# Weight blocks laid out in HBM so that each one is contiguous per partition

## The chip, the cores and the metric

The kernel runs on one core of one Trainium2 chip. Within that core five engines work side by side: TensorE (PE, with its weight loads shown apart as PEld), VectorE (DVE), ScalarE (ACT), GpSimd (POOL) and SyncE (SP). SP does no arithmetic here; it issues DMAs, and nearly all DMAs of this kernel are issued by it, in one queue. Sixteen DMA engines move the data between HBM and the core's SBUF.

The metric is the device time of one execution in microseconds. Before the change the median of three runs is 2130.68 us (2130.02 to 2132.34).

## The reference

One encoder layer is applied to two sequences of 512 tokens by 1024 channels (a prompt and a sample), all in float32:

```
x = x + 0.5 * swiglu(rms_norm(x, ffn1_norm), w_gate, w_up, w_down)     # D_FF = 2816
h = rms_norm(x, mix_norm);  proj = h @ w_in                            # w_in: 1024 x 4880
att = grouped-query attention (8 query heads, 2 key heads, 64 wide, axial rotary, QK norm)
mem = bidirectional mLSTM (4 heads, 128 wide), normed per head, times a sigmoid gate
x = x + (sigmoid(g_att) * (att @ w_up_att) + sigmoid(g_mlstm) * (mem @ w_up_mlstm)) @ w_out
x = x + 0.5 * swiglu(rms_norm(x, ffn2_norm), w_gate, w_up, w_down)
return rms_norm(x, final_norm)
```

`swiglu(x) = (silu(x @ w_gate) * (x @ w_up)) @ w_down`. Columns of `w_in` are, in order, attention q (512), k and v (256), memory q, k and v (512 each), 16 gate columns, the memory's output gate (512) and the two merge gates (1024 each).

## The kernel before

Both sequences are worked on together. The stages in order of time are: the first FFN's gate and up products (to about 440 us), its down product (to about 660 us), the mixing block for one sequence and then the other (to about 1475 us), and the second FFN, gate and up (to about 1865 us) and down (to the end).

Every product keeps float32 accuracy by splitting both operands into a high and a low float32r part and adding three products, high by high, high by low and low by high. So every weight block that is loaded is split once, by an ACT copy (the high part) and a DVE subtraction (the low part), before TensorE can use it.

The gate and up products of an FFN are one 2x2 block product (gate and up against the two sequences, the contraction cut in two halves) done with seven instead of eight block products, so that sums of blocks have to be formed on DVE. The output is walked in 22 steps of 128 columns; `ORDER` (L368) fixes which. A step j takes 128 columns of the gate weight and the same 128 of the up weight. `Up.fetch` (L382) asks for both and `fetch_w` (L188) issues one DMA for each on SP, into a tile `wr` of 128 x 8 x 128 floats (512 KB); four such tiles exist. In HBM the weight is 1024 x 2816 and row-major, so that a partition's 4 KB of such a block lie in eight pieces of 512 bytes.

`gu_left_a`, `gu_left_b` and `gu_left_c` (L253 to L276) turn the two blocks into the seven left operands. The first DVE operation that needs the up block is L263. `gu_rest` (L300) runs the products of a step; each is 12 matmuls at L282. For the first seven of the 22 columns blocks two of the seven products are done early (`Up.begin`, L385) and their results are parked in HBM and fetched again at L400, so in the first 14 steps a step with 5 products alternates with one with 7. The sum at L311 (`u2 = v1 + Y`) writes a ring buffer, and TensorE's next products into the bank Y wait for it.

After every second step `Sides.even` and `Sides.odd` (L348, L353) form the seven right operands of the down product from the two steps' results. `Sides.out` (L340) splits one (L343 on ACT, L344 on DVE) and stores the high and the low part to the DRAM buffer `rbuf` by two DMAs of 256 KB (L345 and L346). With `last=True` the low part is written over the source, so that the source's ring buffer comes free only once that store has landed. L311 of the next step waits for such a buffer; this is the "DMA rbuf<-t" of the profile.

So one SP queue carries, in the order in which the program was scheduled, the stores of the sides, the loads of the next gate and up blocks, the parked results, and in the down stage the loads `rt<-rbuf` of 512 KB each (L457) and the down weights. An SP instruction that waits holds back all that stand behind it.

In the mixing block `load_w` (L208) loads and splits a weight block. `win_cols` (L693) loads 128 columns of `w_in` as 8 x 128; `tok_proj` (L645) loads two row blocks of 512 columns, or for keys and values 256 + 16 columns by two DMAs; `up_unit` (L967) loads 4 x 256 and `out_half` (L1095) 2 x 512.

```
raw = wpool.tile(shape, F32, tag="wr", bufs=4, name=nm("wr"))
for v in views:
    nc.sync.dma_start(raw[:, :, c:c + v.shape[2]], v)      # L195
...
self.v = [w.rearrange("(k p) c -> p k c", p=P) for w in (wg, wu)]
return [fetch_w(self.v[i][:, :, j * P:(j + 1) * P]) for i in which]
```

Of the kernel before, what the change touches and what calls it, by code (L numbers as in the profile page):

```python
# [16 lines left out]
P = 128  # L17
S = 512
D = 1024
KD = D // P  # L20
# [6 lines left out]
def encoder(ctx, tc, I, outs):  # L27
    nc = tc.nc
# [159 lines left out]
    def fetch_w(view):  # L188
        views = view if isinstance(view, list) else [view]
        shape = list(views[0].shape)  # L190
        shape[2] = sum(v.shape[2] for v in views)
        raw = wpool.tile(shape, F32, tag="wr", bufs=4, name=nm("wr"))
        c = 0
        for v in views:
            nc.sync.dma_start(raw[:, :, c:c + v.shape[2]], v)  # L195
            c += v.shape[2]
        return raw
# [18 lines left out]
    V_ = nc.vector  # L216
# [23 lines left out]
        pin(nc.scalar.activation(t[:, 0], src, AF.Copy))  # L240
        pin(V_.tensor_tensor(t[:, 1], src, f(t[:, 0]), op=ALU.subtract))  # L241

    def gu_fetch(wgv, wuv, j):
        cs = slice(j * P, (j + 1) * P)
        return fetch_w(wgv[:, :, cs]), fetch_w(wuv[:, :, cs])

    half = lambda r, i: r[:, i * HK_:(i + 1) * HK_, :]
    part = lambda t, i: (t[:, 0, i], t[:, 1, i])

# [120 lines left out]
    class Up:  # L370


        def __init__(self, xc, wg, wu, rb):
            self.xc, self.rb = xc, rb
            self.v = [w.rearrange("(k p) c -> p k c", p=P) for w in (wg, wu)]
            self.kept = {}
            self.ring = Rings(s=["t2"] * 3, wd=["f2"] * 2, v=["t2"] * 3, h=["t2"] * 5, o=["f2"] * 2 + ["R"] * 2)
            self.ring.rows["o"] += tables(FFN_ROWS)
            self.ring.join("x", "v", "h")
            self.ring.rows["k"], self.ring.at["k"] = self.ring.rows["o"][:2], 0  # L380

        def fetch(self, j, which=(0, 1)):  # L382
            return [fetch_w(self.v[i][:, :, j * P:(j + 1) * P]) for i in which]

        def begin(self, j, W):  # L385

# [237 lines left out]
            tabs.append((cg, sg))  # L624
        tabs.extend((tri, msk))

    w_in = I["w_in"][0]
    win_v = w_in.rearrange("(k p) c -> p k c", p=P)


    held = []
# [1 line left out]
    def go(*units):  # L633
        for load, comp in units:
            held.append((comp, load()))
            while len(held) > 1:
                c, w = held.pop(0)
                c(w)
# [3 lines left out]
            c, w = held.pop(0)  # L642
            c(w)

    def tok_proj(xh, xl, cols, kk, done):  # L645

        N = sum(n for _, n in cols)
        p = []

        def load(k0):  # L650
            return load_w([win_v[:, k0:k0 + kk, c:c + n] for c, n in cols], nc.vector)

        def comp(k0, w):
            wh, wl = w
            if not p:
                p.extend([MM(), MM(), MM(), PO()])
            for kl in range(kk):
                k = k0 + kl
                for b in range(4):
# [21 lines left out]
    def mix(s, xh, xl, before, after):  # L681

        xsrc = lambda k: (xh[:, k, :], xl[:, k, :])
# [7 lines left out]
            return T2(dtype, "f2")  # L691

        def win_cols(c0, done):  # L693
            return proj(win_v[:, :, c0:c0 + P], xsrc, KD, done)


        kv = A([P, 8, S], F32R, "kv")
# [76 lines left out]
        cs = small(96, "cs")  # L774
# [39 lines left out]
        def mem_values():  # L814
            def done(pvv):
                vm = A([P, 2, 4, S], F32R, "Vm")
                for b in range(4):
                    split(pvv[b], vm[:, 0, b, :], vm[:, 1, b, :])
                Vm.append(vm)
            return tok_proj(xh, xl, [(1792, 512)], 2, done)  # L820

        qks = {}

        def mem_qk(h, j):
            def done(pp):
                if j == 0:
                    qks[h] = wpool.tile([P, 4, S], F32R, tag="w8", bufs=4, name=nm("qk"))
                split(pp, qks[h][:, 2 * j, :], qks[h][:, 2 * j + 1, :])
            return win_cols((768, 1280)[j] + h * P, done)

        ogs = {}

        def out_gate(h):
            def done(pp):
                og = T2(F32, "ac")
                nc.scalar.activation(og, pp, AF.Tanh, scale=0.5)
                G_.tensor_scalar(og, og, 1.0, hn[:, h:h + 1], op0=ALU.add, op1=ALU.mult)
                ogs[h] = og
            return win_cols(2320 + h * P, done)

        def q_rope(b):
            qo = rope_apply(qraw[b], rq[0][:, b * 8:(b + 1) * 8], tabs[0], b).rearrange("p (h e) -> p h e", e=DA)
# [6 lines left out]
                nc.scalar.activation(qT[:, g * 4:g * 4 + 4, b * P:(b + 1) * P],  # L849
                                     p.rearrange("p (h t) -> p h t", t=P), AF.Copy)  # L850

        go(*tok_proj(xh, xl, [(512, 256), (2304, 16)], 2, kv_done))
        go(*tok_proj(xh, xl, [(0, 512)], 2, q_done), mem_qk(0, 0))
        yield None
        box()
        gates()
# [90 lines left out]
        def att_gate(d):  # L947
            def done(pp):
                nc.scalar.activation(mg[:, d, :], pp, AF.Tanh, scale=0.5)
            return win_cols(2832 + d * P, done)  # L950

        queue.extend(att_gate(d) for d in range(KD))
        queue.extend(out_gate(h) for h in range(2))
# [11 lines left out]
        wups = {}  # L965

        def up_unit(part, d, src, done):  # L967
            def load():
                if d % 2 == 0:
                    wv = I[("w_up_att", "w_up_mlstm")[part]][0].rearrange("(k p) c -> p k c", p=P)  # L970
                    wups[part, d // 2] = load_w(wv[:, :, d * P:(d + 2) * P], nc.vector)

            def comp(_):
                wu = wups[part, d // 2]
                cl = slice((d % 2) * P, (d % 2 + 1) * P)
                done(proj_w(wu[0][:, :, cl], wu[1][:, :, cl], lambda k: (src[:, k, 0, :], src[:, k, 1, :]), 4))
            return load, comp
# [8 lines left out]
        def mem_gate(d):  # L986
            def done(pp):
                t = ths[d] = T2()
                nc.scalar.activation(t, pp, AF.Tanh, scale=0.5)
            return win_cols(3856 + d * P, done)  # L990

        def merge_mem(d):
            def done(pu):
# [95 lines left out]
        yield None  # L1089


        wov = I["w_out"][0].rearrange("(k p) c -> p k c", p=P)
        rows = A([P, 2, 4, S], F32, "rows") if s else None

        def out_half(h):  # L1095

            p = []

            def comp(k0, w):
                if not p:  # L1100
                    p.extend([MM(), MM(), MM(), PO()])
                for k in (k0, k0 + 1):
                    for b in range(4):
                        bs = slice(b * P, (b + 1) * P)
                        for i, (a, w_) in enumerate(((mh, w[0]), (mh, w[1]), (ml, w[0]))):
                            nc.tensor.matmul(p[b], a[:, k, bs], w_[:, k - k0, :],  # L1106
                                             start=(k == 0 and i == 0), stop=(k == KD - 1 and i == 2))
                if k0 + 2 < KD:
                    return
                for b in range(4):  # L1110
                    xt = rows[:, h, b, :] if s else T2()
                    nc.sync.dma_start(xt, xbuf[s][:, h, b, :])
                    V_.scalar_tensor_tensor(xt, p[b], 0.5, xt, op0=ALU.mult, op1=ALU.add)
                    nc.sync.dma_start(x2buf[s][:, h, b, :], xt)
                    square(xt, ssq2[s][:, h, b:b + 1])

            return [(lambda k0=k0: load_w(wov[:, k0:k0 + 2, h * S:(h + 1) * S], V_), lambda w, k0=k0: comp(k0, w))
                    for k0 in range(0, KD, 2)]

        go(*out_half(0), *out_half(1))  # L1120
# [5 lines left out]
    for _ in range(8):  # L1126
# [3 lines left out]
    rbuf = [[[dpool.tile([P, 2, S], F32, name=f"rbuf{n}_{j}_{m}") for m in range(7)] for j in range(NF // 2)]  # L1130
            for n in range(2)]
    xnbuf = dpool.tile([P, KD, S], F32, name="xnbuf")
    raws = [A([P, 4, D], F32, "raw") for _ in range(2)]
    xc = [None] * 7
    up = Up(xc, I["ffn1_w_gate"][0], I["ffn1_w_up"][0], rbuf[0])
# [96 lines left out]
    for k in range(HK_):  # L1232
# [3 lines left out]
        for t, kk, bank in ((x1l, k, PS), (x1u, k + HK_, PT)):  # L1236
            p = turn(1, kk, [bank])
# [50 lines left out]
    xc = [None] * 7  # L1288
# [14 lines left out]
    rows1 = next(m1)  # L1303


    up = Up(xc, I["ffn2_w_gate"][0], I["ffn2_w_up"][0], rbuf[1])
    raw0 = up.fetch(0)
    W = [gu_left_a(raw0[0])]
    up.begin(0, W[0])
# [68 lines left out]
        'ffn2_w_gate', 'ffn2_w_up', 'ffn2_w_down', 'final_norm']  # L1378


# [17 lines left out]
```

## Time and profile before

| | us |
|---|---|
| median of three runs | 2130.68 (2130.02 to 2132.34) |
| the profiled execution | 2131.81 |
| its span, first to last instruction | 2130.0 |
| TensorE matmul busy | 2071.1 (97%) |
| TensorE weight loads busy | 1689.2 (79%) |
| DVE busy | 1579.5 (74%) |
| ACT busy | 968.5 (45%) |
| DMA queue of SP, share of 16 engines' span | 50.6% |

The profile shows one execution. A row of a timeline gives start and length in us, engine, source line, operation and tiles (`out<-in`, buffer numbers left out); in brackets stands the idle time of the engine just before it and what ended it. The chain of waits is followed back from the last instruction: at each point it names the work, or the DMA, that the next piece waited for. The list of waits adds up, for each engine and line, how long it stood idle for which releaser (us in total, times, longest). The list of DMA issues gives tile and source, count, size and the median time from issue to landing. Stretches ("windows") give busy time with the number of instructions in brackets, for PE, PEld, DVE, ACT and POOL, then the granted clock, the DMA share and GB/s.

### The profile page before, as it was taken

The numbers are of one execution on the slowest core, as the hardware profiler recorded it, in microseconds if no ns is written. First come the engines' busy times: TensorE is split into PE (matmuls) and PEld (weight loads), VectorE is DVE, ScalarE is ACT, GpSimd is POOL, SyncE is SP. The second block draws the span as 40 slices with busy tenths as digits, with TensorE's granted clock in tenths as the row PEclk, the third lists the DMA queues.
The fourth block names the chain that finished last, engine by engine and source line by source line (L and its number), as shares of the span: only waits on it lengthen the run. The fifth ranks groups of instructions, "written<-read, shape, count | busy, mean of one in ns | idle before, by whom it ended". The sixth has DMA issues, their size and how long they took to land.

```text
span 2130.0 us, 26826 instructions
## 1 busy us (share of the span) xinstructions
PE 2071.1 (97%) x9472; PEld 1689.2 (79%) x9472; DVE 1579.5 (74%) x2817; ACT 968.5 (45%) x1739; POOL 104.1 (5%) x110
## 2 busy tenths in 40 slices
PE   6999999999999999999999999999999999999997
PEld 5877788888888777878887887788877778888885
DVE  7888887776696796574668755754978887786686
ACT  6534444442225466454435654544644444442223
POOL 1000000001000110100102001010000000000002
PEclk9999999999999999999999999999999999999998
DMA  8465554389765222333352232454464654479753
GB/s 266 150 197 186 182 196 142 131 303 378 281 219 162 78 71 64 95 103 97 117 159 81 60 90 79 129 178 158 154 197 159 197 165 166 142 261 386 284 207 122
DMA packets 294486, 361.81 MB, mean 170 GB/s; under 512 B 17776, under 2 KB 187776, under 8 KB 293328
## 3 DMA queue, kind: packets, MB, share of 16 engines
q1 hardware_dynamic: 293760, 358.84, 50.6%
q0 software_dynamic: 592, 1.27, 0.3%
q8 instruction: 74, 1.21, 0.2%
q14 instruction: 60, 0.49, 0.1%
HBM read 255.15 MB, written 104.89 MB: 169 GB/s over the span
## 4 chain that ended last, share of the span: by engine, by line
PE 74%; DVE 10%; DMA 6%; issue 6%; ACT 4%; POOL 0%; SPq 0%; DVEq 0%; ACTq 0%; POOLq 0%
PE mm L678 14%; PE pss L282 13%; PE pst L282 8%; PE mm L523 8%; PE mm L282 7%; PE pss L523 4%; PE pst L523 4%; PE mm L662 3%; PE pso L523 3%; DMA rbuf<-t 2%; DMA wr<-in_ffn_w_up_dram 2%; PE pso L932 1%; PE mm L1106 1%; PE pso L1062 1%; DVE w L241 1%
## 5 line engine op out<-in xcount | busy, mean ns | idle before, releaser
L678 PE MATMUL mm<-xh,w 128*128 128x512 f32 x896 | 292.0, 395 | 0.0
L282 PE MATMUL pss<-xc,w 128*128 128x512 f32 x1056 | 258.4, 391 | 12.4 <-DVE t L311 12.4
L282 PE MATMUL mm<-xc,w 128*128 128x512 f32 x1056 | 256.0, 391 | 2.5 <-ACT f L291 2.4
L282 PE MATMUL pst<-xc,w 128*128 128x512 f32 x1056 | 255.4, 390 | 0.0
L282 PEld LDWEIGHTS pss<-xc,w 128*128 128x128 f32 x1056 | 196.6, 188 | 60.4 <-DVE t L311 20.0
L282 PEld LDWEIGHTS mm<-xc,w 128*128 128x128 f32 x1056 | 196.8, 188 | 46.8 <-ACT f L291 6.6
L282 PEld LDWEIGHTS pst<-xc,w 128*128 128x128 f32 x1056 | 197.3, 188 | 43.2 <-ACT t L315 2.5
L203 DVE TENSOR_TENSOR w<-wr,w 128x1024 fp32r<-128x1024 f32 (+1 forms) x112 | 135.9, 1215 | 106.0 <-ACT w L202 100.7
L678 PEld LDWEIGHTS mm<-xh,w 128*128 128x128 f32 x896 | 167.6, 188 | 32.1
L523 PE MATMUL mm<-w,rt 128*128 128x512 f32 x792 | 185.6, 390 | 1.1 <-DMA rt<-rbuf 1.1
L678 PE MATMUL mm<-xl,w 128*128 128x512 f32 x448 | 176.7, 394 | 0.0
L523 PEld LDWEIGHTS mm<-w,rt 128*128 128x128 f32 x792 | 148.4, 188 | 32.5 <-DMA rt<-rbuf 1.8
L240 ACT ACTIVATE w<-t 128x512 fp32r<-128x512 f32 x176 | 107.0, 628 | 122.8 <-DVE t L266 42.0
L202 ACT ACTIVATE w<-wr 128x1024 fp32r<-128x1024 f32 (+1 forms) x112 | 114.4, 1028 | 99.4 <-PE mm L678 29.4
L241 DVE TENSOR_TENSOR w<-t,w 128x512 fp32r<-128x512 f32 x176 | 118.0, 689 | 44.5 <-ACT w L240 41.5
L282 PE MATMUL pss<-xc,f 128*128 128x512 f32 x528 | 128.4, 392 | 0.0
L282 PEld LDWEIGHTS pss<-xc,f 128*128 128x128 f32 x528 | 98.2, 188 | 23.6 <-DVE t L319 3.6
L580 ACT ACTIVATE w<-wr 128x512 fp32r<-128x512 f32 x72 | 44.6, 631 | 132.4 <-PE pso L523 64.3
L580 ACT ACTIVATE w<-t 128x512 fp32r<-128x512 f32 x82 | 51.6, 632 | 115.9 <-PE pst L523 47.3
L678 PEld LDWEIGHTS mm<-xl,w 128*128 128x128 f32 x448 | 84.3, 188 | 15.7
L523 PE MATMUL pss<-w,rt 128*128 128x512 f32 x396 | 94.0, 389 | 0.0
L523 PE MATMUL pst<-w,rt 128*128 128x512 f32 x396 | 93.7, 389 | 0.0
(316 smaller groups left out, 3644.4 us busy)
## 6 DMA issues: line engine op xcount, KB each, us to landing
rt<-rbuf SPq DMA_DIRECT2D x154, 512.0 KB, 5.8
wr<-in_w_in_dram SPq DMA_DIRECT2D x72, 512.0 KB, 3.6
wr<-in_ffn_w_gate_dram SPq DMA_DIRECT2D x56, 512.0 KB, 5.3
rbuf<-tab SPq DMA_DIRECT2D x90, 256.0 KB, 3.2
wr<-in_ffn_w_up_dram SPq DMA_DIRECT2D x44, 512.0 KB, 4.2
rbuf<-t SPq DMA_DIRECT2D x88, 256.0 KB, 3.5
rbuf<-f SPq DMA_DIRECT2D x66, 256.0 KB, 3.2
rbuf<-R SPq DMA_DIRECT2D x64, 256.0 KB, 3.5
```

The source lines that it names most:

```text
L202: pin(nc.scalar.activation(hi, raw, AF.Copy))
L203: pin(lo_eng.tensor_tensor(lo, raw, f(hi), op=ALU.subtract))
L240: pin(nc.scalar.activation(t[:, 0], src, AF.Copy))
L241: pin(V_.tensor_tensor(t[:, 1], src, f(t[:, 0]), op=ALU.subtract))
L282: nc.tensor.matmul(p, a[:, k, :], xt[:, b, k, :], start=(first and k == 0 and i == 0), stop=(k == HK_ - 1 and i == 2), skip_group_check=True)
L523: nc.tensor.matmul(p, r[:, b, d * P:(d + 1) * P], u[:, a, :], start=(first and q == 0 and k == 0), stop=(q == len(us) - 1 and k == 2), ski ...
L580: nc.scalar.activation(hi, src, AF.Copy)
L662: nc.tensor.matmul(p[b][:, :N], a[:, k, bs], w_[:, kl, :], start=(k == 0 and i == 0), stop=(k == KD - 1 and i == 2))
L678: nc.tensor.matmul(p, a[:, k, :], b, start=(k == 0 and i == 0), stop=(k == n - 1 and i == 2))
L932: nc.tensor.matmul(po, Vst[:, kv_, hk, :], w, start=(kv_ == 0 and i == 0), stop=(kv_ == 3 and i == 1))
L1062: nc.tensor.matmul(po, vm[:, a, t, hs_], b, start=(t == 0 and n == 0), stop=(t == 3 and n == 2))
L1106: nc.tensor.matmul(p[b], a[:, k, bs], w_[:, k - k0, :], start=(k == 0 and i == 0), stop=(k == KD - 1 and i == 2))
```

## The change

The host lays the weights out anew with numpy before the program is built (`lay_out`); values are not changed. For each block that the kernel loads, the bytes of one partition become one contiguous run, and the block as a whole becomes contiguous in HBM. The loads take these blocks by index. The 256 + 16 columns of keys and values become one block of 272, so two DMAs become one. The down weights, inputs, constants and all buffers in HBM that the kernel writes itself stay as they were. `gu_fetch`, which nothing called, goes.

```
     def __init__(self, xc, wg, wu, rb):
-        self.v = [w.rearrange("(k p) c -> p k c", p=P) for w in (wg, wu)]
+        self.v = wg, wu
     def fetch(self, j, which=(0, 1)):
-        return [fetch_w(self.v[i][:, :, j * P:(j + 1) * P]) for i in which]
+        return [fetch_w(self.v[i][j]) for i in which]
...
-    w_in = I["w_in"][0]
-    win_v = w_in.rearrange("(k p) c -> p k c", p=P)
+    win_c, win_t = I["w_in_cols"], {n: I[f"w_in_{n}"] for n in ("q", "kv", "mv")}
...
-            return load_w([win_v[:, k0:k0 + kk, c:c + n] for c, n in cols], nc.vector)
+            return load_w(win_t[name][k0 // kk], nc.vector)
...
-            return proj(win_v[:, :, c0:c0 + P], xsrc, KD, done)
+            return proj(win_c[c0], xsrc, KD, done)
...
-        go(*tok_proj(xh, xl, [(512, 256), (2304, 16)], 2, kv_done))
+        go(*tok_proj(xh, xl, "kv", 272, 2, kv_done))
...
-                    wups[part, d // 2] = load_w(wv[:, :, d * P:(d + 2) * P], nc.vector)
+                    wups[part, d // 2] = load_w(I[("w_up_att", "w_up_mlstm")[part]][d // 2], nc.vector)
...
-            return [(lambda k0=k0: load_w(wov[:, k0:k0 + 2, h * S:(h + 1) * S], V_), lambda w, k0=k0: comp(k0, w))
+            return [(lambda k0=k0: load_w(wov[h, k0 // 2], V_), lambda w, k0=k0: comp(k0, w))
...
+def lay_out(given):
+    def blocks(w, rows, cols):
+        w = w.reshape(w.shape[0] // (rows * P), rows, P, w.shape[1] // cols, cols)
+        return np.ascontiguousarray(w.transpose(3, 0, 2, 1, 4))
+    for n in (1, 2):
+        for part in ("gate", "up"):
+            name = f"ffn{n}_w_{part}"
+            given[name] = blocks(given[name][0], KD, P)[:, 0]
+    w = given.pop("w_in")[0]
+    given["w_in_cols"] = blocks(np.concatenate([w[:, 768:1792], w[:, 2320:]], axis=1), KD, P)[:, 0]
+    given["w_in_q"] = blocks(w[:, :512], 2, 512)[0]
+    given["w_in_kv"] = blocks(np.concatenate([w[:, 512:768], w[:, 2304:2320]], axis=1), 2, 272)[0]
+    given["w_in_mv"] = blocks(w[:, 1792:2304], 2, 512)[0]
+    for name in ("w_up_att", "w_up_mlstm"):
+        given[name] = blocks(given[name][0], 4, 2 * P)[:, 0]
+    given["w_out"] = blocks(given["w_out"][0], 2, S)
```

In the scheduled program the order of the instructions on TensorE, ScalarE and GpSimd is the same as before. On DVE two neighbouring instructions of the mixing block's start change places (L145 and L203). On SP the order is the same but for the eight DMAs of 16 gate columns, which are gone; the semaphores that the later DMAs report on are numbered differently, since they are dealt out in turn.

More of the change, by code (lines that the diff above doesn't have):

```diff
@@ L241, in w_pair @@
         pin(V_.tensor_tensor(t[:, 1], src, f(t[:, 0]), op=ALU.subtract))
-    def gu_fetch(wgv, wuv, j):
-        cs = slice(j * P, (j + 1) * P)
-        return fetch_w(wgv[:, :, cs]), fetch_w(wuv[:, :, cs])
     half = lambda r, i: r[:, i * HK_:(i + 1) * HK_, :]
@@ L643, in flush, with tok_proj @@
             c(w)
-    def tok_proj(xh, xl, cols, kk, done):
-        N = sum(n for _, n in cols)
+    def tok_proj(xh, xl, name, N, kk, done):
         p = []
         def load(k0):
-            return load_w([win_v[:, k0:k0 + kk, c:c + n] for c, n in cols], nc.vector)
+            return load_w(win_t[name][k0 // kk], nc.vector)
         def comp(k0, w):
@@ L819, in done @@
                 Vm.append(vm)
-            return tok_proj(xh, xl, [(1792, 512)], 2, done)
+            return tok_proj(xh, xl, "mv", 512, 2, done)
         qks = {}
@@ L828, in done @@
                 split(pp, qks[h][:, 2 * j, :], qks[h][:, 2 * j + 1, :])
-            return win_cols((768, 1280)[j] + h * P, done)
+            return win_cols(4 * j + h, done)
         ogs = {}
@@ L838, in done @@
                 ogs[h] = og
-            return win_cols(2320 + h * P, done)
+            return win_cols(8 + h, done)
         def q_rope(b):
@@ L850, in q_rope @@
                                      p.rearrange("p (h t) -> p h t", t=P), AF.Copy)
-        go(*tok_proj(xh, xl, [(512, 256), (2304, 16)], 2, kv_done))
-        go(*tok_proj(xh, xl, [(0, 512)], 2, q_done), mem_qk(0, 0))
+        go(*tok_proj(xh, xl, "kv", 272, 2, kv_done))
+        go(*tok_proj(xh, xl, "q", 512, 2, q_done), mem_qk(0, 0))
         yield None
@@ L949, in done @@
                 nc.scalar.activation(mg[:, d, :], pp, AF.Tanh, scale=0.5)
-            return win_cols(2832 + d * P, done)
+            return win_cols(12 + d, done)
         queue.extend(att_gate(d) for d in range(KD))
@@ L969, in load @@
                 if d % 2 == 0:
-                    wv = I[("w_up_att", "w_up_mlstm")[part]][0].rearrange("(k p) c -> p k c", p=P)
-                    wups[part, d // 2] = load_w(wv[:, :, d * P:(d + 2) * P], nc.vector)
+                    wups[part, d // 2] = load_w(I[("w_up_att", "w_up_mlstm")[part]][d // 2], nc.vector)
             def comp(_):
@@ L989, in done @@
                 nc.scalar.activation(t, pp, AF.Tanh, scale=0.5)
-            return win_cols(3856 + d * P, done)
+            return win_cols(20 + d, done)
         def merge_mem(d):
@@ L1089, in mix @@
         yield None
-        wov = I["w_out"][0].rearrange("(k p) c -> p k c", p=P)
+        wov = I["w_out"]
         rows = A([P, 2, 4, S], F32, "rows") if s else None
@@ L1134, in encoder @@
     xc = [None] * 7
-    up = Up(xc, I["ffn1_w_gate"][0], I["ffn1_w_up"][0], rbuf[0])
+    up = Up(xc, I["ffn1_w_gate"], I["ffn1_w_up"], rbuf[0])
     xins = [I[n][0] for n in ("x_prompt", "x_sample")]
@@ L1303, in encoder @@
     rows1 = next(m1)
-    up = Up(xc, I["ffn2_w_gate"][0], I["ffn2_w_up"][0], rbuf[1])
+    up = Up(xc, I["ffn2_w_gate"], I["ffn2_w_up"], rbuf[1])
     raw0 = up.fetch(0)
@@ L1378 @@
         'ffn2_w_gate', 'ffn2_w_up', 'ffn2_w_down', 'final_norm']
+def lay_out(given):
+    import numpy as np
+    def blocks(w, rows, cols):
[13 more added lines that the diff above has]
+    given["w_out"] = blocks(given["w_out"][0], 2, S)
+    return given
 def kernel(**inputs):
@@ L1388 @@
     given = {n: _np.ascontiguousarray(inputs[n]) for n in _INS}
+    given = lay_out(given)
     given.update(host_consts())
```

## The prediction

> **What bounds the kernel now.** I read the page first, then who waited for whom, then the chain of waits in the stage that this points to.
>
> ```profile
> span 2130.0 us, 26826 instructions
> PE 2071.1 (97%) x9472; PEld 1689.2 (79%) x9472; DVE 1579.5 (74%) x2817; ACT 968.5 (45%) x1739; POOL 104.1 (5%) x110
> DMA packets 294486, 361.81 MB, mean 170 GB/s; under 512 B 17776, under 2 KB 187776, under 8 KB 293328
> q1 hardware_dynamic: 293760, 358.84, 50.6%
> ```
>
> TensorE is busy for 2071.1 of 2130.0 us, and the change takes no matmul away. A faster load can win at most what TensorE stands idle, 58.9 us, and of that only what a weight load causes. The DMA engines are half idle, so bytes per second over the whole run are not the limit; single transfers that somebody waits for are. TensorE's waits are these:
>
> ```profile
> PE pss L1147 <- DVE raw L1195: 13.7, 2, 11.3
> PE pss L282 <- DVE t L311: 12.4, 14, 2.3
> PE pst L848 <- DVE t L581: 4.4, 4, 1.8
> ...
> PE mm L523 <- DMA rt<-rbuf: 1.1, 1, 1.1
> ```
>
> The first is the norm of the inputs at the start, which needs the x rows and no weight. The third is arithmetic of the attention, as are most of those left out. The last is a load that isn't changed. The second is the gate and up stage of both FFNs: 14 waits, 12.4 us in all, for the DVE sum at L311. What that sum waits for, from the list of waits of DVE:
>
> ```profile
> DVE t L263 <- DMA wr<-in_ffn_w_up_dram: 29.7, 33, 1.8
> DVE t L311 <- DMA rbuf<-t: 14.0, 13, 2.8
> DVE R L1187 <- DMA raw<-in_x_prompt_dram: 6.3, 3, 3.4
> ```
>
> L311 waits for a store (its ring buffer must have been written out), and earlier in the same step DVE waits at L263 for the up block. The chain of waits over one such place, and SP's queue there:
>
> ```profile
> 173.85 2.73 PE pst L282 x12
> ...
> 178.81 0.68 DVE w L241
> 179.50 0.61 DVE t L344
> ...
> 180.12 4.09 DMA rbuf<-t
> ...
> 184.24 0.70 DVE t L311
> ...
> 184.98 1.19 PE pss L282 x4
> ```
>
> ```profile
> 173.20 0.41 SPq L195 DMA_DIRECT2D wr<-in_ffn_w_up_dram  x1
> ...
> 176.99 0.40 SPq L346 DMA_DIRECT2D rbuf<-t  x1
> 177.43 0.78 SPq L195 DMA_DIRECT2D wr<-in_ffn_w_gate_dram  x1
> 180.12 0.32 SPq L346 DMA_DIRECT2D rbuf<-t  x1
> ```
>
> The store issued at 180.12 takes 4.09 us. In the queue there stand ahead of it the next gate block (177.43), stores, and the up block (173.20). Both loads are of the changed kind. At 1547.74 and 1554.60 the same chain shows the two transfers one behind the other:
>
> ```profile
> 1547.74 4.30 DMA wr<-in_ffn_w_up_dram
> ...
> 1554.60 5.16 DMA rbuf<-t
> ```
>
> **The change part by part.** *Gate and up blocks (56 + 44 loads).* Each load keeps its 512 KB but its 1024 pieces of 512 bytes become 128 of 4 KB. The trace has 4 KB rows of the same total size already: the loads of `rt`. First the gate, then the up blocks, then `rt`:
>
> ```profile
> L195 SPq DMA_DIRECT2D wr<-in_ffn_w_gate_dram x56: 367/392/4948, 2.6 to 1843.2; - x56
> DMA to landing us min/median/max: 3.7/5.3/10.5
> L195 SPq DMA_DIRECT2D wr<-in_ffn_w_up_dram x44: 367/384/3274, 14.8 to 1849.8; - x44
> DMA to landing us min/median/max: 3.7/4.2/8.6
> L457 SPq DMA_DIRECT2D rt<-rbuf x154: 319/320/975, 445.5 to 2082.8; - x154
> DMA to landing us min/median/max: 3.1/5.8/10.1
> ```
>
> The medians say little, since `rt` loads come in bursts and queue behind each other. The shortest landings compare alike: 3.7 against 3.1 us, 0.6 us less a load. The start of the kernel gives a second view, where the queue is full: from 13 to 16 us it moves x rows of 4 KB, from 18.3 to 22 us weight blocks of 512-byte pieces.
>
> ```profile
> 13.00:16.00 3.00, 0.00 (x0) 0.00 (x0) 2.59 (x14) 0.78 (x1) 0.00 (x0) 1.00 1.03 410
> 18.30:22.00 3.70, 3.70 (x24) 3.57 (x23) 3.61 (x5) 3.70 (x8) 0.00 (x0) 1.00 1.16 290
> ```
>
> At 410 GB/s a block of 524,288 bytes streams in 1.28 us, at 290 in 1.81 us: 0.53 us less. So 0.6 us a load is my value; the ends are 0 (the landing is all latency; a loss is the last of the rivals) and 0.9, from the 243 GB/s that a stretch with an up block inside a step shows below (2.16 us a block, against 1.28).
>
> ```profile
> 1549.30:1551.00 1.70, 1.70 (x9) 1.39 (x9) 1.70 (x4) 0.00 (x0) 0.00 (x0) 1.00 0.91 243
> ```
>
> On the path of one wait lie two loads, the up block (by L263 and by the queue) and the gate block (by the queue ahead of the store), so 1.2 us can come off each wait, and no more than the wait itself. Of the 14 waits four are longer:
>
> ```profile
> 184.98 3.92 PE L282 MATMUL pss<-xc,w 128*128 128x512 f32 x16 [1.30 <-DVE t L311]
> 1560.52 3.92 PE L282 MATMUL pss<-xc,w 128*128 128x512 f32 x16 [2.29 <-DVE t L311]
> 1595.00 3.93 PE L282 MATMUL pss<-xc,w 128*128 128x512 f32 x16 [1.28 <-DVE t L311]
> 1629.59 3.92 PE L282 MATMUL pss<-xc,w 128*128 128x512 f32 x16 [1.39 <-DVE t L311]
> ```
>
> They keep 0.10 + 1.09 + 0.08 + 0.19 = 1.5 us, and 12.4 - 1.5 = 10.9 us go. What is late next? A pair of steps lasts 34.49 us in the worst of these stretches:
>
> ```profile
> 150.49:184.98 34.49, 33.19 (x144) 26.80 (x145) 28.12 (x44) 14.46 (x24) 0.00 (x0) 1.00 0.59 190
> ```
>
> DVE works 28.12 us of it. Even when TensorE's 33.19 us leave no gap, DVE has 5 us to spare, ACT more. So TensorE itself is next, and no new wait takes the gain.
>
> The Trainium skill, "DMA: Bandwidth & Descriptors", section "Why small descriptors are slow (HBM only)", charges a fixed 3 cycles or so to each piece, 32 bytes a cycle. By that, 512 bytes cost 19 cycles where the share of a 4 KB piece costs 16.4, so a block would stream only about 0.2 us faster, an estimate from that page; then two loads give 0.4 us a wait, at most 14 x 0.4 = 5.6 us, and 2125.1. The two stretches above speak for more.
>
> *Up blocks, early.* SP itself is held while it issues these loads, up to 4948 and 3274 ns at the start of the kernel by the rows above. Fewer pieces hold it less. Nothing of TensorE waits for SP there except through x, so I take 0. The x rows land ahead of the gate blocks in the same queue; DVE waits 6.3 us for them in three pieces, the first of 3.4 until anything can have landed. The other 2.9 bound what a lighter queue could give, and a change of sign has the same bound at most; I take 0.
>
> *Mixing block: `w_in`, `w_up_att`, `w_up_mlstm`, `w_out`.* 0.
>
> ```profile
> L203 DVE TENSOR_TENSOR w<-wr,w 128x1024 fp32r<-128x1024 f32 (+1 forms) x112 | 135.9, 1215 | 106.0 <-ACT w L202 100.7
> L202 ACT ACTIVATE w<-wr 128x1024 fp32r<-128x1024 f32 (+1 forms) x112 | 114.4, 1028 | 99.4 <-PE mm L678 29.4
> wr<-in_w_in_dram SPq DMA_DIRECT2D x8, 16.0 KB, 3.7
> ```
>
> The splits of these blocks wait for each other and, first, for TensorE to free a buffer, not for the load; matmuls at L678 cover it. Were that cover gone, a shorter load would help, not hurt. The eight small DMAs of gate columns go, with 0.4 us of SP each, which nobody waits for: 0. Their partner's rows become 2176 bytes, between sizes that the trace has. On DVE two neighbours change places (L145 and L203); one may wait for the other's 0.7 to 1.2 us, eight loads early in the block, so within 1 us either way; I take 0. The renumbered semaphores make a DMA wait for another one eight issues back, which is old by then: 0.
>
> *The sum.* The profiled execution took 2131.81 us, 1.81 beside its span; 2131.8 - 10.9 = 2120.9. It lies 1.1 above the median of the runs, 2130.68, so against that 2119.8.
>
> **The rivals.** *One load only.* If the store gains from the gate block alone, because the up block's lead is lost in the wait for L344, 0.6 us a wait remain: at most 14 x 0.6 = 8.4, less for waits that are shorter, some 7.5, and 2123. For it: in the chain at 180.12 the up load doesn't stand. Against it: the queue between 173 and 184 holds both.
>
> *All of it and the start.* With 0.9 us a load only the wait of 2.29 keeps 0.5; with the x rows' 2.9 us too, 12.4 - 0.5 + 2.9 = 14.8, and 2115.9. Against it: the x rows go first.
>
> *Nothing changes.* A load might cost what its latency and bytes cost, whatever its pieces; 0 a load, 2130.7. For it: the queue is half idle, and the 3.7 us of a lone block are more than twice the time that its bytes stream. Against it: 290 against 410 GB/s. The Trainium skill's page "DMA: Bandwidth & Descriptors", section "Specifications", puts line rate at 512 bytes and more; by that rule this case holds, and the two stretches disagree.
>
> *Slower.* Sixteen engines now read rows that lie side by side in one block of 512 KB, instead of pieces 11 KB apart. If those collide in HBM and a block lands later than 3.7 us, each load is added where it is now taken off. A block that lands 0.6 us later makes each of the 14 waits 1.2 us longer: 16.8 us, 2147.5; it decides from the point where a block lands 0.15 us later than now (14 x 0.3 = 4.2 us). Against it: x rows and `rt` lie in just that way and go at 410 GB/s.
>
> **How the numbers follow.** Forecast 0.50, one load only 0.20, all of it 0.13, nothing 0.10, slower 0.07. About 0.2%, 4.3 us, is what a measurement here can tell from no change: the first three are all faster by more, 0.83; same 0.10; slower 0.07. The range goes from the third case's 2115 to 2129, which lets in part of the case without change; what is left out is under 0.15. The forecast alone: 2117.5 to 2122.
>
> **What would show it.** Right: the shortest landing of gate and up blocks near 3.1 us; some 140,000 packets fewer than the 294486 of now (56 gate, 44 up and 56 blocks of `w_in`, 896 each); DVE's 29.7 us at L263 and 14.0 at L311 mostly gone; TensorE's 12.4 us at L311 under 2.5; the other waits of TensorE the same. Wrong: landings that stay at 3.7; a store in front of L311 that still takes 4 to 5 us; TensorE's waits moving to another line, above all to products at L282 that wait for ACT or for a weight split that comes late.

## The result and the profile after

The changed kernel takes 2124.55 us, the median of eight runs (2122.64 to 2124.94); beside them the kernel before took 2129.69 (eight runs). The ratio is 0.9971, with a 95% interval of 0.9962 to 0.9980: 5.1 us of gain on the medians, where 10.9 were forecast. The profiled execution took 2124.45 us.

First the head of the page of the changed kernel:

```profile
span 2122.7 us, 26809 instructions
...
PE 2070.4 (98%) x9472; PEld 1687.7 (80%) x9472; DVE 1581.2 (74%) x2817; ACT 968.5 (46%) x1739; POOL 107.2 (5%) x110
...
DMA packets 141270, 361.81 MB, mean 170 GB/s; under 512 B 15600, under 2 KB 15616, under 8 KB 140112
```

The work is the same: the same bytes, the same 9472 matmuls and the same busy time. TensorE stood idle for 2130.0 - 2071.1 = 58.9 us before and for 2122.7 - 2070.4 = 52.3 us now, 6.6 us less. The packets fell from 294486 to 141270.

The diff takes four lines away above the gate and up stage, so the sum at L311 is L307 now, the matmuls at L282 are L278, L263 is L259 and L346 is L342. The list of waits of TensorE, kernel after (total us, times, longest):

```profile
PE pss L1140 <- DVE raw L1188: 13.6, 2, 11.2
PE pss L278 <- DVE t L307: 6.5, 8, 2.0
PE pst L842 <- DVE t L577: 4.9, 4, 2.1
```

Of the 6.6 us, 12.4 - 6.5 = 5.9 come off the waits for this one sum. The start and the attention stand as before. So the place was right, and the question is why about half of the waits is left. The list of waits of DVE, kernel after:

```profile
DVE t L259 <- DMA wr<-in_ffn_w_up_dram: 26.1, 29, 1.8
DVE t L307 <- DMA rbuf<-t: 11.4, 13, 2.5
```

Both are still there: 29.7 became 26.1, 14.0 became 11.4. The loads, from the views of the gate tile and of the up tile of the kernel after:

```profile
L195 SPq DMA_DIRECT2D wr<-in_ffn_w_gate_dram x56: 327/333/853, 2.6 to 1836.2; - x56
DMA to landing us min/median/max: 3.4/4.3/6.8
L195 SPq DMA_DIRECT2D wr<-in_ffn_w_up_dram x44: 328/333/1755, 11.1 to 1842.8; - x44
DMA to landing us min/median/max: 3.4/4.1/4.6
```

The shortest landing went from 3.7 to 3.4 us, not to 3.1. The gate block's median fell from 5.3 to 4.3 us, the up block's by 0.1. SP itself is held less by the issue of a load, at most 853 ns where it was 4948 (gate) and 1755 where it was 3274 (up).

The chain of waits shows a place where the change did what it should (kernel after, second FFN):

```profile
1548.74 2.12 DMA rbuf<-tab
...
1552.17 3.68 DMA rbuf<-t
...
1555.87 0.70 DVE t L307
...
1556.61 3.49 PE pss L278 x14
```

Before, an up load of 4.30 us and a store of 5.16 us stood one behind the other here. Now the load is out of the chain and the store takes 3.68 us; TensorE's wait fell from 2.29 to 0.66 us. At the place of the first FFN that the prediction showed, next to nothing was won:

```profile
178.07 3.98 DMA rbuf<-t
...
182.07 0.70 DVE t L307
...
182.81 1.20 PE pss L278 x4
```

The store in front of the sum takes 3.98 us (4.09 before), and TensorE's wait went from 1.30 to 1.27 us. Of TensorE's timeline, kernel after, the two longest and two later rows that wait for the sum:

```profile
182.81 3.94 PE L278 MATMUL pss<-xc,w 128*128 128x512 f32 x16 [1.27 <-DVE t L307]
217.99 3.92 PE L278 MATMUL pss<-xc,w 128*128 128x512 f32 x16 [1.95 <-DVE t L307]
...
1556.61 3.72 PE L278 MATMUL pss<-xc,w 128*128 128x512 f32 x15 [0.66 <-DVE t L307]
...
1624.37 3.92 PE L278 MATMUL pss<-xc,w 128*128 128x512 f32 x16 [0.92 <-DVE t L307]
```

The ordinary waits of the first FFN, 0.4 to 0.9 us at 116, 150, 252 and 286 us, are gone. What is left has come together in a few places.

### The profile page after: what moved, and what is told of

Same layout as the page of the kernel before. It is cut to its first block, busy times and chain, and to the rows that moved or that the text cites. A ratio compares the mean times of both kernels' runs of the same rounds, so it can differ in the third digit from the quotient of the medians.

```text
span 2122.7 us, 26809 instructions
## 1 busy us (share of the span) xinstructions
PE 2070.4 (98%) x9472; PEld 1687.7 (80%) x9472; DVE 1581.2 (74%) x2817; ACT 968.5 (46%) x1739; POOL 107.2 (5%) x110
## 2 busy tenths in 40 slices
DMA packets 141270, 361.81 MB, mean 170 GB/s; under 512 B 15600, under 2 KB 15616, under 8 KB 140112
## 3 DMA queue, kind: packets, MB, share of 16 engines
q0 software_dynamic: 592, 1.27, 0.3%
q8 instruction: 74, 1.21, 0.2%
## 4 chain that ended last, share of the span: by engine, by line
PE 81%; DVE 10%; ACT 4%; DMA 4%; issue 2%; POOL 0%; SPq 0%; ACTq 0%; DVEq 0%; POOLq 0%
PE pss L278 15%; PE mm L672 14%; PE pst L278 9%; PE mm L519 8%; PE mm L278 7%; PE pst L519 4%; PE pss L519 4%; PE mm L656 4%; PE mm L1099 3%; PE pso L519 3%; DMA rbuf<-t 2%; PE pso L926 2%; PE pso L656 1%; PE pso L1055 1%; PE pst L919 1%
## 5 line engine op out<-in xcount | busy, mean ns | idle before, releaser
L278 PE MATMUL pss<-xc,w 128*128 128x512 f32 x1056 | 258.1, 391 | 6.7 <-DVE t L307 6.5
L278 PE MATMUL mm<-xc,w 128*128 128x512 f32 x1056 | 256.2, 391 | 3.0 <-ACT f L287 2.6
L278 PE MATMUL pst<-xc,w 128*128 128x512 f32 x1056 | 255.4, 390 | 0.0
L278 PEld LDWEIGHTS pss<-xc,w 128*128 128x128 f32 x1056 | 196.5, 188 | 54.2 <-DVE t L307 13.6
L278 PEld LDWEIGHTS mm<-xc,w 128*128 128x128 f32 x1056 | 196.7, 188 | 47.7 <-ACT f L287 6.9
L278 PEld LDWEIGHTS pst<-xc,w 128*128 128x128 f32 x1056 | 197.3, 188 | 43.2 <-ACT t L311 2.5
L203 DVE TENSOR_TENSOR w<-wr,w 128x1024 fp32r<-128x1024 f32 (+1 forms) x112 | 135.9, 1215 | 105.5 <-ACT w L202 104.8
L278 PE MATMUL pss<-xc,f 128*128 128x512 f32 x528 | 128.5, 392 | 0.0
L278 PEld LDWEIGHTS pss<-xc,f 128*128 128x128 f32 x528 | 98.2, 188 | 23.6 <-DVE t L315 3.6
```

The source lines that it names most:

```text
L203: pin(lo_eng.tensor_tensor(lo, raw, f(hi), op=ALU.subtract))
L278: nc.tensor.matmul(p, a[:, k, :], xt[:, b, k, :], start=(first and k == 0 and i == 0), stop=(k == HK_ - 1 and i == 2), skip_group_check=True)
```

## The experiments

Three theories were to be told apart first. A: both loads of a step are on the path, so gate and up each bring half. B: only the gate block counts, because it stands in SP's queue ahead of the store that the sum waits for. C: it isn't the pieces of 512 bytes but that a block lies in one stretch of HBM. Beside these stood the question whether the mixing block has a part at all. Each ratio below is to the kernel before, run beside the kernel in question.

**The FFN weights alone, and the mixing block alone.** In the first kernel `w_in`, `w_up_att`, `w_up_mlstm` and `w_out` are loaded as before, in the second the gate and up weights. The first is made from the kernel before, the second from the changed kernel:

```
first:
-            self.v = [w.rearrange("(k p) c -> p k c", p=P) for w in (wg, wu)]
+            self.v = wg, wu
...
-            return [fetch_w(self.v[i][:, :, j * P:(j + 1) * P]) for i in which]
+            return [fetch_w(self.v[0][j] if i == 0 else self.v[1][j]) for i in which]
...
second:
-            self.v = wg, wu
+            self.v = [w.rearrange("(k p) c -> p k c", p=P) for w in (wg, wu)]
...
-            return [fetch_w(self.v[i][j]) for i in which]
+            return [fetch_w(self.v[i][:, :, j * P:(j + 1) * P]) for i in which]
```

> Only the gate and up blocks of the two FFNs are laid out anew; the blocks of w_in, w_up_att, w_up_mlstm and w_out are loaded as before. If all of the gain comes from the FFN loads (theory), it is 5 us faster than the kernel before, about 2124.5, and TensorE's wait for the sum `u2 = v1 + Y` falls from 12.4 to about 6.5 us. If the mixing block's loads carry part of it (rival), it is at most 3 us faster.

> Only the blocks of the mixing block (w_in, w_up_att, w_up_mlstm, w_out) are laid out anew, gate and up blocks as before. Theory: no change, within 1 us of the kernel before, TensorE's wait for `u2 = v1 + Y` stays at about 12. Rival (the mixing block shares the gain): 2 us faster or more.

The FFN weights alone: 2124.95 us, ratio 0.9975 (0.9963 to 0.9986). The mixing block alone: 2129.95 us, ratio 0.9996 (0.9987 to 1.0005). TensorE's waits for the sum, first with the FFN weights alone, then with the mixing block alone:

```profile
PE pss L282 <- DVE t L311: 6.2, 9, 1.3
```

```profile
PE pss L278 <- DVE t L307: 11.0, 14, 2.4
```

The first is close to the changed kernel's wait, the second to that of before. All that can be measured comes from the gate and up blocks; what the 112 loads of the mixing block are worth can't be told from nothing (0.9987 to 1.0005).

**Gate alone, up alone.** One of the two FFN weights has the new layout, all else is as before:

```
gate alone:
+            return [fetch_w(self.v[0][j] if i == 0 else self.v[1][0].rearrange("(k p) c -> p k c", p=P)[:, :, j * P:(j + 1) * P]) for i in which]
up alone:
+            return [fetch_w(self.v[0][0].rearrange("(k p) c -> p k c", p=P)[:, :, j * P:(j + 1) * P] if i == 0 else self.v[1][j]) for i in which]
```

> Only the gate blocks of the FFNs are laid out anew, the up blocks as before. Theory, the queue: the gain comes from the gate block that stands in the queue ahead of the store that the sum waits for, so nearly all of it remains, 4 to 5 us faster than before (2125). Rival, both loads alike (as the prediction had it): half remains, 2.5 us faster. Second rival, the up block's lead alone: no gain.

> Only the up blocks of the FFNs are laid out anew, the gate blocks as before. Theory, the queue: 0 to 1 us faster than before, since an up block lands in 4.1 instead of 4.2 us. Rival, both loads alike: 2.5 us faster. Second rival, the up block's lead alone: 5 us faster.

Gate alone: 2125.47 us, ratio 0.9974 (0.9963 to 0.9986). Up alone: 2130.37 us, ratio 0.9992 (0.9982 to 1.0002). The lists of waits, gate alone:

```profile
PE pss L282 <- DVE t L311: 7.7, 7, 2.1
...
DVE t L263 <- DMA wr<-in_ffn_w_up_dram: 35.0, 33, 3.0
...
DVE t L311 <- DMA rbuf<-t: 5.6, 7, 1.5
```

and up alone:

```profile
PE pss L282 <- DVE t L311: 11.5, 13, 2.6
...
DVE t L263 <- DMA wr<-in_ffn_w_up_dram: 23.6, 26, 1.4
...
DVE t L311 <- DMA rbuf<-t: 16.6, 12, 3.1
```

These rows say how the two waits of DVE in one step hang together. With a faster up block DVE waits 29.7 - 23.6 = 6.1 us less at L263, comes to the sum sooner, and there waits 16.6 - 14.0 = 2.6 us more for the store, which has not become faster; TensorE's 12.4 us fall to 11.5, and the time can't be told from no change. (Where the rest of the 6.1 us goes, these lists don't say.) With a faster gate block DVE waits 5.3 us longer at L263 and 8.4 us less for the store, and TensorE's wait falls by 4.7 us. The store ends the wait, and the block in the queue ahead of it is the gate's. By the waits A falls and B stands. The times lean the same way, though less clearly: half of the gain of the FFN weights would be a ratio of about 0.9987, just outside the interval of gate alone and inside that of up alone.

**Pieces or place.** The gate and up blocks are each one stretch of 512 KB in HBM, but in the old order of rows, so that a partition still has eight pieces of 512 bytes. The rest is as in the changed kernel.

```
-            given[name] = blocks(given[name][0], KD, P)[:, 0]
+            given[name] = np.ascontiguousarray(given[name][0].reshape(D, NF, P).transpose(1, 0, 2))
...
-            return [fetch_w(self.v[i][j]) for i in which]
+            return [fetch_w(self.v[i][j].rearrange("(k p) c -> p k c", p=P)) for i in which]
```

> As the changed kernel, but the gate and up blocks of 512 KB are laid out row by row: the block is contiguous in HBM as a whole, and a partition still gets it in eight pieces of 512 bytes. If the number of pieces makes the difference (theory), the gate block lands as before (shortest 3.7, median 5.3 us) and the time is that of before, 2129.5. If it is that the block lies together in HBM (rival), it lands as in the changed kernel (3.4 and 4.3 us), 2124.5.

2129.12 us, ratio 0.9990 (0.9980 to 1.0000); the wait and, from the gate tile's view, the issue:

```profile
PE pss L278 <- DVE t L307: 10.6, 12, 1.7
```

```profile
L195 SPq DMA_DIRECT2D wr<-in_ffn_w_gate_dram x56: 367/393/4878, 2.6 to 1840.5; - x56
DMA to landing us min/median/max: 3.8/4.4/6.4
```

The wait is near that of before, and SP is held up to 4878 ns as before. C falls: the pieces bring the gain. The ratio's interval touches 1 and overlaps a little with that of the FFN weights alone, so this rests on the wait as much as on the time. The median landing of the gate block, 4.4 us, is already near the changed kernel's 4.3, though, so this median doesn't rank the kernels; it mixes lone loads with those behind stores.

**What the rest of the wait is made of: a fetch of instructions.** The trace holds a third kind of traffic, the queue q8 of the page, 74 packets in the whole run (page of the kernel after):

```profile
q8 instruction: 74, 1.21, 0.2%
```

That is 16 KB a packet (1.21 MB over 74). It is also 256 instructions a packet, when TensorE's 9472 matmuls and as many weight loads are spread over the 74. In the packet records of the kernel after they start 17 to 37 us apart, 28 at the median, and each takes 0.9 to 1.8 us. By the queue's share of 0.2% that is the time of one of the 16 DMA engines. In the kernel after, such packets lie at 177.8 and 212.4 us, 3.7 and 3.6 us ahead of the start of the two longest waits (181.54 and 216.03), just when the store must be moved. Those at 1553.1, 1585.7 and 1791.9 us stand 2.1 to 4.1 us ahead of three more waits, the one at 1613.1 stands 10.4 us ahead of the wait of 0.92; these six waits hold 6.0 of the 6.5 us. In the kernel before, packets at 180.1, 1557.2, 1589.5 and 1617.7 us stand 3.6, 1.0, 4.3 and 10.5 us ahead of its four longest waits.

What a fetch does to a store can be read from the landings, which the trace gives in sixteen parts for each DMA. Over the stores to `rbuf` in the gate and up stages of the kernel after, as far as all parts are on record, the last part lands 0.97 us behind the fifteenth at the median where a fetch runs meanwhile (11 stores), and 0.04 us where none does (122 stores); in the kernel before it is 0.99 us (14) and 0.10 us (118). Of the six waits three stand behind such a store, those issued at 212.37, 1585.94 and 1789.12 us: the last part is 2.1, 0.5 and 1.5 us behind the fifteenth, and TensorE waits 1.95, 0.43 and 0.77 us.

With a packet every 28 us a step has one near it by chance too, so they were also moved. For that, more matmuls that compute nothing that is used go ahead of everything:

```
-    for _ in range(8):
+    for _ in range(48):
```

> The changed kernel with 48 instead of 8 warming matmuls at the start, while TensorE stands idle; they shift the times at which TensorE's next 16 KB of instructions are fetched, by 80 of 256 instructions or some 9 us earlier, and nothing else. Theory: the waits that are left (6.5 us) stand where such a fetch, one packet of about 1 us on one DMA engine, falls 2 to 5 us ahead of the sum and holds up that engine's share of the store. Then the waits at 182 and 217 us go, one may come at 115, those of the second FFN go or become short, and the sum falls to 2 to 3 us, the time to about 2121. Rival, the fetch has no part in it: waits at the same places as in the changed kernel, 6.5 us, and 2124.5.

2123.80 us, ratio 0.9965 (0.9953 to 0.9978), against the 0.9971 of the changed kernel no difference that can be told. The edit adds 80 matmuls and as many weight loads, and the packets came some 20 us earlier, more than the 9 us expected. TensorE's timeline, three of the rows that wait for the sum:

```profile
280.07 3.96 PE L278 MATMUL pss<-xc,w 128*128 128x512 f32 x16 [0.52 <-DVE t L307]
...
1654.10 3.92 PE L278 MATMUL pss<-xc,w 128*128 128x512 f32 x16 [1.25 <-DVE t L307]
...
1688.33 3.94 PE L278 MATMUL pss<-xc,w 128*128 128x512 f32 x16 [1.02 <-DVE t L307]
```

The waits at 182, 216, 1556 and 1590 us are gone, and these three start 4.1, 2.9 and 3.5 us behind the packets' new times (275.5, 1650.0 and 1683.8 us). So the places of the longest waits move with the fetches. But the list gives

```profile
PE pss L278 <- DVE t L307: 4.8, 8, 1.2
```

and not 2 to 3 us, beside 6.5 and (below) 5.7 in two profiles of the changed kernel: the fetches come at other steps rather than at none.

**The gate block out of SP's queue.** If the gate block ahead of the store is the trouble, another queue might free the store. GpSimd issues the gate loads of the steps, 43 of 56:

```
-    def fetch_w(view):
+    def fetch_w(view, q=None):
...
-            nc.sync.dma_start(raw[:, :, c:c + v.shape[2]], v)
+            (q or nc.sync).dma_start(raw[:, :, c:c + v.shape[2]], v)
...
+            return [fetch_w(self.v[i][j], nc.gpsimd if i == 0 and len(which) == 2 else None) for i in which]
```

> The changed kernel with the gate loads of the 22 steps issued by GpSimd instead of SP, so that the store no longer stands behind the gate block in SP's queue. Theory, the queue: the store lands in 2 to 3 us, TensorE's wait for `u2 = v1 + Y` falls from 6.5 to 1 to 2 us, and the time to about 2120. Rival, the DMA engines themselves are the limit whoever issues: the wait stays at about 6.5 and the time at 2124.5. Third case: the gate block lands so much later from GpSimd that the split of the gate block comes late, and it is slower than the changed kernel.

2151.95 us, ratio 1.0098 (1.0084 to 1.0112), slower than both kernels. The waits, and the store in the chain at the place of the longest wait:

```profile
PE pss L278 <- DVE t L307: 26.4, 15, 3.4
...
DVE t L307 <- DMA rbuf<-t: 26.8, 15, 3.7
```

```profile
218.59 5.95 DMA rbuf<-t
```

SP does not hold the store back (it is issued at 218.59, when DVE ends the split), and yet it needs 5.95 us. GpSimd began to issue the gate load at 214.72. In the packet records the first sixteen packets of this load take 0.65 to 2.35 us each, and none of SP's queue starts between 217.0 and 218.5 us. This place is the extreme. Over the 43 loads the first sixteen packets take 0.31 us at the median; a fetch of instructions, which begins at 220.46 us, runs during this store too; and at a more ordinary place the store issued at 109.54 us takes 4.29 us. Over the whole run the gate blocks land later, at 5.8 us in the median where it was 4.3, and DVE waits 26.8 us for the store where it was 11.4. No engine waits for a gate block itself, so it isn't a late split as in the third case. A second queue does not pass the first one by; both use the same 16 engines. How the engines divide their time between the two is not shown, and the loss is explained in part only: TensorE stands idle 15.0 us longer than in the changed kernel, but its 9472 matmuls are also busy 11.7 us longer, which no wait explains.

**The gate block behind the store.** In six places of each FFN the gate load is put behind the store that the sum waits for, by an edge that only orders the two in SP's queue. It is done in the new layout and, as its partner, in the old one; beside them the changed kernel ran again.

```
+                tc.add_manual_dep(load.ins, behind.ins.name, mybir.DependencyInfo(
+                    mybir.DependencyClass.NoSync, mybir.DependencyReason.DATA), reason="behind the store")
...
+        def fetch(self, j, which=(0, 1), behind=None):
+            return [fetch_w(self.v[i][j], None if i else behind) for i in which]
...
+            self.mark = self.out(T1, t1, True)
...
+                    raw = self.fetch(ORDER[i + 2], behind=mark if i % 2 and i > 1 else None) if i + 2 < NF else None
```

> The changed kernel, with SP's order altered in six places of each FFN: the gate load that stood just ahead of the store which the sum `u2 = v1 + Y` waits for now stands just behind it. Theory, the queue: the store lands in 2 to 3 us, TensorE's wait for that sum falls from 6.5 to 1 us or less (a rest where an instruction fetch falls in), the time from 2124.5 to 2118 to 2120. Rival (the store is slow for what the engines do besides, wherever the gate block stands): wait and time stay.

> The kernel before, in the old layout, with the same alteration of SP's order. Theory, the queue: the wait of 12.4 us falls to 1 to 2 us too, since what counted was the gate block in front of the store; the time falls from 2130 to about 2120, and the layout is then worth 1 us at most beside it. Rival (the layout itself is worth its 5 us wherever the block stands): it stays 5 us slower than the run with the new layout and the same order.

> The changed kernel once more, on the same chip as the two runs with the altered order, so that they can be compared: 0.997 of the kernel before, 6.5 us of wait for `u2 = v1 + Y`.

| kernel | us | ratio to before | TensorE's wait for the sum | DVE's wait for the store |
|---|---|---|---|---|
| new layout, gate block behind the store | 2124.03 | 0.9966 (0.9953 to 0.9978) | 5.1 | 3.8 |
| old layout, gate block behind the store | 2126.69 | 0.9985 (0.9976 to 0.9994) | 7.2 | 2.9 |
| the changed kernel again | 2122.71 | 0.9964 (0.9951 to 0.9976) | 5.7 | 10.4 |

The waits for the sum and for the store, first in the old layout with the gate block behind the store, then in the changed kernel run again:

```profile
PE pss L285 <- DVE t L314: 7.2, 12, 1.4
...
DVE t L314 <- DMA rbuf<-t: 2.9, 6, 1.0
```

```profile
PE pss L278 <- DVE t L307: 5.7, 7, 1.6
...
DVE t L307 <- DMA rbuf<-t: 10.4, 12, 2.3
```

The waits with the new layout and the gate block behind the store:

```profile
PE pss L281 <- DVE t L310: 5.1, 8, 1.1
...
DVE t L262 <- DMA wr<-in_ffn_w_up_dram: 22.3, 28, 1.5
...
DVE t L310 <- DMA rbuf<-t: 3.8, 7, 1.0
```

and its chain at one of the longest places:

```profile
1613.20 5.58 DMA wr<-in_ffn_w_up_dram
...
1619.41 1.28 DVE w L244 x2
1620.69 0.60 DVE t L343
1621.30 0.60 DVE t L360
...
1622.42 1.29 DVE t L343 x2
1623.71 0.61 DVE t L310
...
1624.36 3.70 PE pss L281 x15
```

In the old layout the new order alone takes 4.3 us off the median (3.2 by the ratio), so the place in the queue is a cause by itself. The new layout adds about 2.7 us to that (4.0 by the ratios), with overlapping intervals. Both theories of the queue promised more: 1 us or less of TensorE's wait in the new layout, 1 to 2 us in the old one, and 5.1 and 7.2 stayed. In the new layout the order wins nothing on top: DVE's wait for the store fell from 10.4 to 3.8 us, TensorE's for the sum only from 5.7 to 5.1. The chain shows what is late next in this place. No store is in it. The up block takes 5.58 us, counted from the start of its issue, and SP's queue there shows that the issue itself was held:

```profile
1613.20 1.58 SPq L195 DMA_DIRECT2D wr<-in_ffn_w_up_dram  x1
```

In the kernel after, the issue of the up block at 171.06 us took 0.41 us. A fetch of 16 KB begins at 1613.2 us and takes 1.37 us; the block's first packets start at about 1615.5 us. After the landing DVE goes through its operations in order (the splits at L244 and L343, the sums between them) and comes to L310 when TensorE already waits. So a fetch can reach the sum by the up block too, 10 us later. This is no single case: in ten of the twelve profiles of this document the longest issue of a gate or up load after the kernel's start, 1.2 to 2.1 us, is that of an up load at which a fetch begins within 0.12 us. In nine of them it stands between 1609 and 1618 us; in the run with the fetches moved it stands at 1711.09 us, with the moved fetch. The four waits of 0.85 us and more in this run all have a fetch 1.8 to 10.0 us ahead of them, and hold 3.9 of the 5.1 us.

## Why the prediction was right in part

*The place: right.* 5.9 of the 6.6 us that TensorE stands idle less lie in the waits for the sum at L311; no other wait changed by more than 1.1 us, and these went both ways. With the FFN weights alone the whole gain is there; the mixing block, the eight gate-column DMAs and the two DVE operations are worth 0, as put. So are the x rows at the start (13.7 and 13.6 us).

*The packets: right*, 294486 - 141270 = 153216 fewer, against some 140,000.

*The gain of one load: too high.* The step "0.6 us less a load" took the shortest landing of `rt` for that of a gate block of the same pieces. The changed blocks land in 3.4 us at the shortest, 0.3 less than before, half of the term. Alone in the queue a block of 512 KB streams in 2.1 to 2.3 us with pieces of 512 bytes and in 2.0 to 2.2 us with pieces of 4 KB, by the packet records. The comparison of the two stretches (410 against 290 GB/s) was one of a full queue. The medians don't settle the price: 4.3 us for the changed gate block, but 4.4 with its pieces of 512 bytes kept. What was measured on the path is 5.9 / 14 = 0.42 us a wait, between the 0.3 of a load alone and the 0.53 of the full queue; which of the two a store behind the block feels, no run shows.

*Two loads on the path of each wait: wrong.* This is the step that failed. The up block was counted because it stands earlier in the same chain. The run with up alone shows that its lead hardly reaches TensorE (6.1 us won at L263, 2.6 of them lost again in the wait for the store, 0.9 won by TensorE) and that the time stays the same within the interval; the run with gate alone has all of the gain in time and 4.7 of the 5.9 us in the wait. This is the rival "one load only". Its time was 2123 and the measured one is 2124.55; its price of 0.6 a load was too high as well, but its condition held.

*What is late next: wrong in part.* The view of 34.49 us with DVE busy for 28.12 was taken to mean that DVE has 5 us to spare. It has them over a pair of steps, but not between the up block's landing and the sum: there it has its operations in order, and where the up block came late, in the run with the gate block behind the store, a wait of 1.1 us stayed with no store in its chain. The sum over a stretch said nothing of the order within it.

*The four longer waits.* They were read as more of the same wait and left 1.5 us. They, and the six that hold most of what is left, stand behind a fetch of instructions. The places moved with the fetches in the run with more matmuls ahead, and where a fetch runs the last of a store's sixteen parts lands about 1 us late. In three waits, 3.15 of the 6.5 us together, that delay is as long as the wait or longer; no run was without the fetches, so how much of the rest is theirs stays open.

*The Trainium skill's estimate*, "DMA: Bandwidth & Descriptors", section "Why small descriptors are slow (HBM only)", gave 0.2 us a load and 2125.1. The 0.3 us measured for a load alone lies nearer to it than to 0.6. Its time is within 0.6 us of the measured one, but that sum counted both loads, which the runs contradict; a cheaper load twice and a dearer one once come out alike. The rule of the Trainium skill's page "DMA: Bandwidth & Descriptors", section "Specifications", by which pieces of 512 bytes would run at line rate, nearly holds here for the stream of a load alone (2.1 to 2.3 against 2.0 to 2.2 us) and does not hold for the kernel's time: eight pieces of 512 bytes a partition give a ratio of 0.9990 to the kernel before, one of 4 KB gives 0.9971.

*The rivals on the other side.* No gate or up block lands later than before (shortest, median and longest), so "slower" had no ground; "all of it and the start" needed 0.9 us a load, which no row shows.

## What to carry to other kernels

When a transfer stands in a chain of waits, ask which wait ends last and count only what stands in the queue ahead of that one; a transfer that merely comes earlier in the chain may give its gain back at the next wait. A load has no single price: the shortest landing of a lone one, the median and the rate of a full queue gave 0.3, 1.0 and 0.5 us here, and 0.4 us a wait were measured; so put a range on it. And the busy share of an engine over a stretch doesn't say that it has time between two given events; follow its order there.

## What was not expected of the hardware

The loads of instructions are traffic too: packets of 16 KB, 17 to 37 us apart, each 0.9 to 1.8 us long. A store that is spread over all engines lands late by about the length of such a packet: its last sixteenth came 0.97 us behind the others at the median with a fetch beside it, and 0.04 us without. The issue of a load that meets the start of a fetch took 1.2 to 2.1 us in ten of twelve profiles, and moved with the fetch; elsewhere 0.41 us was seen. Loads issued by GpSimd did not spare SP's queue: a store took 4.29 us at an ordinary place and 5.95 at the worst, where for 1.5 us no packet of SP's queue started. And pieces of 512 bytes hold the issuing engine: at the start of the kernel SP stood up to 4948 ns at one load of 1024 pieces (4878 with the pieces kept and the blocks contiguous), and about 610 ns at most at one of 128.
